# An encoder of two layers on one core: 128-row score products, the shared SBUF port in the second ordering, and the softmax's division on two heads' output

## The chip, the core and the metric

The kernel runs on one core of one Trainium2 chip. The core has five engines with queues of their own: TensorE (PE in the profile, with its weight loads shown apart as PEld), VectorE (DVE), ScalarE (ACT), GpSimd (POOL) and SyncE (SP), which here issues the transfers. The metric is device time in microseconds (us) from launch to end. Each engine takes its instructions strictly in the order in which they were issued to it; it waits for other engines by semaphores.

## The reference, cut to what matters

`x` is 256 tokens by 1024, float32. Each of two layers does this:

```python
h = rmsnorm(x, n1)
qa, ka, va, qb, kb, vb = split(h @ w_in)
# A: 8 query heads of 64 dims on 2 key/value heads, every token with every token
s = einsum('bqkgd,bskd->bkgqs', q, k) * scale
p = softmax(s); ya = einsum('bkgqs,bskd->bqkgd', p, v)
# B: 8 heads, three dilated windows, merged by their softmax denominators
y = concat(rmsnorm(ya, out_norm_a), rmsnorm(yb, out_norm_b))
x = x + y @ w_out
u = square(relu(rmsnorm(x, n2) @ w_mlp_in))
x = x + u @ w_mlp_out
```

A final rmsnorm ends the trunk. For B the kernel adds, to the scores, the logarithm of how many of the three windows a key is in; then one softmax does for all three.

## The kernel before, in words

**Products in split parts.** A float32 factor is held as two parts, `hi` (rounded to TensorE's fp32r) and `lo` (the rest). A product is three matmuls: hi·hi, hi·lo, lo·hi. Weights arrive by DMA in `wraw`, chunk by chunk into a ring of 4096 columns; `prep_piece` makes `whi` (a copy by ACT or DVE) and `wlo` (a subtraction by DVE, or by DVE or POOL for the chunks of the projections in `POOLK`, not for those of the MLP) in rings of 8192 columns, in pieces of mostly 640 or 384 columns. `block` is one such product of 128 weight columns with 256 tokens.

**Stages of a layer.** (1) q and k of A, outermost over the eight blocks of the model dimension. (2) V of all heads, with tokens on the partitions; between its products stand five `hooks` that finish q and k of A. (3) Attention of 16 heads, one `score(k)`, `turn(k-1)`, `pv(k-2)` at a time, with products between them that don't need it: `fill_pair` (q and k of a pair of B's heads) and `fill_wa` (A's part of the output projection). (4) B's part of the output projection (`fill_wb`, on banks 1, 5, 6 and 7), residual, second norm. (5) the MLP. In layer 1 the last product has its tokens on the partitions, and the final norm closes it.

**One head.** `QS[i]` holds a head's q with the hi part on 64 partitions and the lo part on the other 64. `k_split` writes a head's k: `ks[0]` has the hi part on both halves (two ACT copies), `ks[1]` has the lo part on one half alone (a DVE subtraction). `score` makes, for each half `th` of the queries, a matmul with 128 rows (q hi and q lo against k hi) and one with 64 rows (q hi against k lo). Then come the row maximum (DVE), the exponentials with their sums `ls` (ACT), `li` = 1/`ls` (DVE), and two instructions that scale the probabilities `p` by `li`, on POOL, DVE or ACT. `turn` transposes `p` on TensorE (four 128x128) and splits it into `h` (ACT) and `l` (DVE). `pv` multiplies by V; at the second head of a pair it adds the hi and lo rows into `y` (two DVE additions, after two ACT copies), sums its squares (POOL) and writes `yh` and `yl` for the output projection.

**What sets the order.** All engine calls go to a `Sequencer`, which records each instruction with its data dependences and an estimated duration (`cost`), and issues them at the end (`issue`) in the order of a list schedule. `order` runs twice. The first run chooses the engine where several can do a step; `PEN` holds penalties in ns by kind. The second run, with the engines fixed, gives the order of issue. `record` marks instructions that use the SBUF port shared by DVE and POOL: DVE's with two inputs in SBUF, DVE's SBUF-to-SBUF copies and scalings, and every POOL instruction that reads a tile. In the first run two such instructions may not overlap; for the second run `issue` empties this mark, so that they may. The order alone is changed by this: the semaphores come from the data. All engine instructions carry one source line (L368), so the profile's groups are told apart by the names of their tiles.

Of the kernel before, what the change touches and what calls it, by code (L numbers as in the profile page):

```python
# [19 lines left out]
NRAW = 4096     # columns of weights as they come  # L20
NHI = 8192      # and split
# [6 lines left out]
NIN0 = 3                              # pairs of ff blocks in the K-outer start of the MLP  # L28
LAG = 2
N_PAIR = 16  # L30
# what an engine's end counts more, in the choice among several, per kind of instruction
PEN = {"": {"POOL": -700}, "norm": {"POOL": -450, "ACT": 300}, "rot": {"POOL": -500}, "hi": {"DVE": 300}}


def plan():
    """The weights in chunks of some columns, in the order in which TensorE takes them."""
    out = []
    for l in range(L):
        out += [(("A", l, kb), 640) for kb in range(8)]
        out += [(("V", l, kb), 640) for kb in range(8)]  # L40
        out += [(("B", l, p, i), 1024) for p in range(4) for i in range(2)]
        out += [(("WA", l, i), 1024) for i in range(4)]
        out += [(("WB", l, p), 1024) for p in range(4)]
        out += [(("IK", l, kb), 256 * NIN0) for kb in range(8)]
# [63 lines left out]
def tables():  # L108
    """Constants that depend on shapes alone: rotary cosines and signed sines on
    [dim of two heads, token], the logarithms (times 8) of how many of the dilated  # L110
    patterns a key is in, the identity, and sums over a head or all."""
    f = np.float32
    tok = np.arange(S)
    d = np.arange(128) % 64
    fa = (f(10000.0) ** (-np.arange(16, dtype=f) / f(16))).astype(f)
    pos = np.where((d < 32)[:, None], (tok // 64)[None], (tok % 64)[None]).astype(f)
    ang = (pos * fa[d % 16][:, None]).astype(f).astype(np.float64)
    ca, sa = np.cos(ang), np.sin(ang) * np.where(d % 32 < 16, -1, 1)[:, None]
    fb = (f(500000.0) ** (-np.arange(8, dtype=f) / f(8))).astype(f)
# [16 lines left out]
class Sequencer:  # L136
    """Takes a kernel's instructions in program order, keeps what that order says
    of their data, and issues them in the order of a list schedule: each engine takes,
    of what is ready for it, what has the longest way to the end."""

    # from the end of one engine's instruction to the start of another's that waits for it
# [14 lines left out]
    def __getattr__(self, name):  # L156
        several = {"DP": ("DVE", "POOL"), "PDA": ("POOL", "DVE", "ACT"), "AD": ("ACT", "DVE")}
        if name not in ("PE", "ACT", "DVE", "POOL", "SP", *several):
            raise AttributeError(name)
        return _Recorder(self, several.get(name, (name,)))  # L160

    @staticmethod
    def form(e, method, args, kw):
        """An engine's instruction for what several engines can do."""
# [12 lines left out]
    def regions(ap, psum):  # L177
        """Where an access lies: partitions and spans of the free axis (a whole PSUM bank)."""
# [12 lines left out]
    def cost(e, method, outs, ins, kw):  # L191
# [6 lines left out]
        if e == "PE":  # L198
            f32 = ins[0].dtype == F32
            if kw.get("is_transpose") or method == "transpose":  # L200
                return 109
            return max(110, 1.7 * n) if f32 else max(109, 0.423 * n)
# [17 lines left out]
    def record(self, engines, method, args, kw):  # L220
# [28 lines left out]
        if engines == ("SP",):  # L249
            # the loads in program order  # L250
# [3 lines left out]
        # the SBUF port that DVE and Pool share  # L254
# [6 lines left out]
    def order(self):  # L261
# [31 lines left out]
        while done < n:  # L293
# [10 lines left out]
            if len(ops[i][0]) > 1:  # L304
                # the engine that ends it first
# [20 lines left out]
    def justify(self, start, end, succ):  # L326
        """Moves all instructions as late as they may be, then as early: gaps close."""
# [3 lines left out]
        for back in (True, False):  # L331
            busy = {e: [] for e in (*self.eng, "PORT")}     # spans, counted from this pass's beginning
# [28 lines left out]
    def issue(self):  # L361
        # once with the shared port, for the choice of engines, and once without
        self.order()
        self.ops = [([x for x in o[0] if x[0] == e], *o[1:5], {}, *o[6:]) for o, e in zip(self.ops, self.on)]
# [15 lines left out]
def trunk(ctx: ExitStack, tc: tile.TileContext, x, wts, prm, tab, fin, out):  # L380
    nc = tc.nc
    sq_ = Sequencer(nc)
    PE, ACT, DVE, POOL, SP, DP, PDA, AD = sq_.PE, sq_.ACT, sq_.DVE, sq_.POOL, sq_.SP, sq_.DP, sq_.PDA, sq_.AD
# [16 lines left out]
    # ---------------------------------------------------------------- tiles  # L400
# [21 lines left out]
    KA = [[T(f"ka{i}{s}", [128, S], F32R) for s in range(2)] for i in range(2)]  # L422
# [3 lines left out]
    tq = T("tq", [128, 2, S])             # gain-folded sines of q and k  # L426
    tb = T("tb", [128, 2, S])             # rs-folded tables of B
# [16 lines left out]
    # ------------------------------------------------------------- weights  # L444
# [6 lines left out]
    def places(total):  # L451
        """Each chunk's place in a circular buffer, and the last chunk that it overwrites."""
# [23 lines left out]
    def prep_piece():  # L476
        """Splits a piece of the next chunk, if its place is free."""
# [27 lines left out]
    def wgt(key, a, n, last=True):  # L505
        """(hi, lo) of n columns from a on in a chunk; with `last`, their last use."""
# [23 lines left out]
    def rowbc(c2, o):  # L530
        """o [128, 256] <- c2 [token, th] along the free axis on every partition."""
# [8 lines left out]
    def sums(l, ps):  # L540
        """From column sums of squares of x: mean square + eps, and its power -1/2."""
# [11 lines left out]
    # ---------------------------------------------------------------- start  # L553
    DVE.memset(ssx[:, 0:128], 0.0)
    # TensorE's clock rises while it waits for x
# [10 lines left out]
    DVE.memset(one, 1.0)  # L566
    x3 = x.rearrange("p (a b) -> p a b", a=KB)
# [46 lines left out]
    def norm_x(l):  # L614
        """norm's scale along the tokens, from the squares' sums."""
# [8 lines left out]
    # ---------------------------------------------------------------- layer  # L624
    for l in range(L):
        gA, gA2, gK, gK2 = P(l, 16), P(l, 17), P(l, 18), P(l, 19)
        # gain-folded tables
# [3 lines left out]
        # ---- q and k of A, K-outer behind the split of h  # L631
# [7 lines left out]
        # ---- V of all heads, tokens on the partitions, with the rest of A's q, k between  # L639
# [17 lines left out]
        def k_split(kh, kst_):  # L657
            """kst_[head][hi, lo]: each a head's 64 rows twice."""
# [15 lines left out]
        cq = cqt.rearrange("p (t h) -> p t h", t=2)   # scale of q's scores / 8  # L674
# [78 lines left out]
        # ---- attention of the 16 heads, with the products that don't need it between  # L753
# [31 lines left out]
        def heads(k):  # L785
            """stationary q, moving k (hi, lo) and the V pair of head k of 16."""
# [6 lines left out]
        def score(k):  # L793
            q, ks, _ = heads(k)
            a = slice(64 * (k % 2), 64 * (k % 2) + 64)
            b = v2(bank[k % 2])
            for th in range(2):
                mm(b[:, th], q[:, th * 128:(th + 1) * 128], ks[0], True, False)
                mm(b[:, th], q[a, th * 128:(th + 1) * 128], ks[1][a], False, True)
# [20 lines left out]
            for th in range(2):  # L820
                sq_.kind = "norm"
                PDA.scale(p[:, th], p[:, th], li[:, th:th + 1])
                sq_.kind = ""
# [16 lines left out]
        def pv(k):  # L840
# [10 lines left out]
            # rows of hi and lo parts together: a pair's y^T  # L851
# [7 lines left out]
            DVE.tensor_tensor(out=y[64:128], in0=bb[64:128, 1], in1=t_[64:128], op=ALU.add)  # L859
            ss = ssA if pr < 4 else ssB  # L860
# [68 lines left out]
        # ---- residual, norm2, MLP  # L929
# [37 lines left out]
        def mlp_out_t(ps_, banks=None):  # L967
            """W2 stationary: out^T."""
# [9 lines left out]
        # the last product's sums: half of the tokens, columns, bank  # L978
        outs = ((0, 0, 512, 1), (0, 512, 1024, 5), (1, 0, 512, 6), (1, 512, 768, 7), (1, 768, 1024, 4))

        def mlp_out_n(ps_, which=outs):
            """u^T stationary: out with tokens on the partitions."""
# [19 lines left out]
        def seed():  # L1002
            """The sums of the last product start from x, turned back."""
# [74 lines left out]
```

## Time and profile before

| | us |
|---|---|
| median of 3 runs | 632.05 |
| the three runs | 629.9, 632.05, 635.52 |
| span of the profiled execution (first to last instruction) | 630.3 |

For the profiled execution the span alone is given; it lies between the lowest of the runs and their median.

How to read the lines that follow: a group line gives engine, operation, output tile<-input tiles, shapes and xcount, then busy us and the mean ns of one, then the idle time of the engine before them and what ended it. A matmul's line gives `rows*columns` of the weights and then the moving shape. A line of the stretches view gives, for A:B in us, the length, the busy time of PE, PEld, DVE, ACT and POOL, each with its instruction count, then the granted TensorE clock as a share of full speed, the DMA engines' busy share and GB/s. A timeline line gives start, duration, engine, operation and tiles, and in brackets the engine's idle time before it with what ended that. Matmul durations overlap, since the engine is pipelined: the distance from start to start says what one costs.

### The profile page before, as it was taken

What the parts mean: (1) busy time and instruction counts of PE and PEld (TensorE: products, weight loads), DVE (VectorE), ACT (ScalarE), POOL (GpSimd) and SP (SyncE); (2) the same over time, 40 slices, a digit from 0 to 9 for tenths busy, and PEclk for the clock granted to TensorE, in tenths of its full rate; (3) what the DMA queues carried; (4) which work ended last, traced back from release to release, by engine and by line L of the source; (5) the groups of instructions that cost most, each with busy time, mean ns of one, the idle gap of its engine ahead of it and who ended that gap; (6) DMA issues with size and microseconds to landing.
All of it is one profiled execution on the core that took longest, in us unless ns stands there. A gap on an engine that the chain in (4) does not pass through costs nothing.

```text
span 630.3 us, 11899 instructions
## 1 busy us (share of the span) xinstructions
PE 611.6 (97%) x4500; PEld 576.6 (91%) x4500; DVE 483.9 (77%) x873; ACT 353.4 (56%) x723; POOL 181.9 (29%) x179
## 2 busy tenths in 40 slices
PE   8989999989999999999999999999999999999996
PEld 8988987989999999999999888898989999999995
DVE  6898899998986566666588879887988766667632
ACT  6567877865544444434464687786654444434412
POOL 1486885841000000000035766667300000000000
PEclk9979999999999999999999999999999999999999
DMA  7833111346674554645444301025568554544501
GB/s 262 275 150 134 68 68 34 130 139 201 251 251 167 203 186 151 222 177 178 141 151 134 135 35 68 34 74 173 158 242 297 204 205 156 221 180 149 186 1 67
DMA packets 29865, 98.58 MB, mean 156 GB/s; under 512 B 3440, under 2 KB 3952, under 8 KB 29808
## 3 DMA queue, kind: packets, MB, share of 16 engines
q1 hardware_dynamic: 29808, 97.82, 44.3%
q8 instruction: 35, 0.57, 0.3%
q14 instruction: 22, 0.18, 0.1%
HBM read 96.76 MB, written 1.05 MB: 155 GB/s over the span
## 4 chain that ended last, share of the span: by engine, by line
PE 65%; DVE 11%; issue 2%; ACT 1%; POOL 1%; POOLq 0%; ACTq 0%; DVEq 0%
PE bank L368 65%; DVE wlo L368 2%; DVE f L368 2%; DVE hl L368 2%; DVE qs L368 1%; DVE hst L368 1%; DVE xT L368 1%; DVE l L368 1%; DVE pr L368 1%; DVE kbt L368 0%; POOL sm L368 0%; ACT f L368 0%; ACT pr L368 0%; POOL f L368 0%; DVE yA__82 L368 0%
## 5 line engine op out<-in xcount | busy, mean ns | idle before, releaser
L368 ACT ACTIVATE whi<-wraw 128x640 fp32r<-128x640 f32 (+3 forms) x312 | 192.9, 643 | 171.3 <-PE bank L368 113.0
L368 DVE TENSOR_TENSOR wlo<-wraw,whi 128x640 fp32r<-128x640 f32 (+3 forms) x296 | 221.0, 777 | 64.7 <-ACT whi L368 63.5
L368 PE MATMUL bank<-hh,whi 128*128 128x256 f32 x784 | 222.4, 285 | 0.7 <-ACT whi L368 0.7
L368 PE MATMUL bank<-hl,whi 128*128 128x256 f32 x784 | 222.5, 285 | 0.6 <-DVE hl L368 0.5
L368 PE MATMUL bank<-hh,wlo 128*128 128x256 f32 x784 | 221.2, 285 | 0.1
L368 PEld LDWEIGHTS bank<-hh,whi 128*128 128x128 f32 x784 | 149.2, 191 | 2.4 <-ACT whi L368 1.2
L368 PEld LDWEIGHTS bank<-hl,whi 128*128 128x128 f32 x784 | 148.1, 189 | 1.4 <-DVE hl L368 1.2
L368 PEld LDWEIGHTS bank<-hh,wlo 128*128 128x128 f32 x784 | 147.3, 189 | 0.6 <-DVE wlo L368 0.3
L368 POOL TENSOR_TENSOR wlo<-wraw,whi 128x384 fp32r<-128x384 f32 (+1 forms) x49 | 66.8, 1375 | 161.1 <-DMA wraw<-in_w_dram 149.7
L368 PE MATMUL bank<-l,whi 128*128 128x256 f32 x256 | 72.4, 283 | 0.0
L368 PE MATMUL bank<-h,wlo 128*128 128x256 f32 x256 | 72.2, 282 | 0.0
L368 PE MATMUL bank<-h,whi 128*128 128x256 f32 x256 | 71.3, 280 | 0.0
L368 POOL TENSOR_TENSOR sm<-sm,mhalf 128x2 f32<-128x2 f32 (+2 forms) x12 | 11.8, 986 | 183.8 <-DVE sm L368 183.8
L368 PE MATMUL bank<-wlo,h 128*128 128x512 f32 (+1 forms) x160 | 56.1, 350 | 0.0
L368 PE MATMUL bank<-whi,l 128*128 128x512 f32 (+1 forms) x160 | 55.9, 349 | 0.0
L368 PE MATMUL bank<-whi,h 128*128 128x512 f32 (+1 forms) x160 | 55.8, 349 | 0.0
L368 PEld LDWEIGHTS bank<-h,whi 128*128 128x128 f32 x256 | 48.4, 190 | 0.0
L368 PEld LDWEIGHTS bank<-h,wlo 128*128 128x128 f32 x256 | 48.0, 188 | 0.0
L368 PEld LDWEIGHTS bank<-l,whi 128*128 128x128 f32 x256 | 47.9, 187 | 0.1
L368 POOL TENSOR_TENSOR ssx<-ssx,f 128x512 f32<-128x512 f32 (+1 forms) x22 | 27.6, 1253 | 48.7 <-ACT f L368 37.3
L368 ACT ACTIVATE h<-f 128x512 fp32r<-128x512 f32 x32 | 20.2, 631 | 28.1 <-DVE f L368 28.1
L368 DVE CAST whi<-wraw 128x640 fp32r<-128x640 f32 (+1 forms) x33 | 14.8, 452 | 26.9 <-PE bank L368 25.6
(113 smaller groups left out, 994.8 us busy)
## 6 DMA issues: line engine op xcount, KB each, us to landing
wraw<-in_w_dram SPq DMA_DIRECT2D x148, 512.0 KB, 3.7
wraw<-in_w_dram SPq DMA_DIRECT2D x31, 320.0 KB, 3.3
wraw<-in_w_dram SPq DMA_DIRECT2D x16, 384.0 KB, 3.3
tabt<-in_t_dram SPq DMA_DIRECT2D x1, 768.0 KB, 7.5
xT<-in_x_dram SPq DMA_DIRECT2D x1, 512.0 KB, 7.0
tabt<-in_f_dram SPq DMA_DIRECT2D x1, 512.0 KB, 7.0
out_dram<-f SPq DMA_DIRECT2D x1, 512.0 KB, 2.6
out_dram<-f SPq DMA_DIRECT2D x2, 256.0 KB, 2.2
```

The lines of the kernel that those rows point to most:

```text
L368: getattr(self.eng[e], method)(*args, **kw)
```

## The change

Four edits:

1. **Score products of 128 rows.** The half of `ks[1]` that held nothing is zeroed once, at the start, by four POOL memsets (for this the four `ka` tiles become one tile `KAt`), and the second score matmul runs over all 128 rows.
2. **The division.** The two scalings of `p` go. `li` is instead copied (DVE, SBUF to SBUF) for two heads into a 128x256 tile `cw`, 64 columns to each head; two TensorE transposes put it on the partitions of `y` in bank 7, and a DVE product scales `y`, before its squares are taken. The kind "norm" and its penalties go with it.
3. **The port kept in the order.** `issue` no longer empties the mark, so the second ordering too keeps DVE's and POOL's port instructions apart.
4. **A cost.** The estimated duration of an fp32r matmul of n columns goes from 0.423 n to 4 + 0.449 n ns (for 256 columns from 108 to 119).

```diff
+PEN = {"": {"POOL": -700}, "rot": {"POOL": -500}, "hi": {"DVE": 300}}
...
-            return max(110, 1.7 * n) if f32 else max(109, 0.423 * n)
+            return max(110, 1.7 * n) if f32 else max(109, 4 + 0.449 * n)
...
     def issue(self):
         self.order()
-        self.ops = [([x for x in o[0] if x[0] == e], *o[1:5], {}, *o[6:]) for o, e in zip(self.ops, self.on)]
+        self.ops = [([x for x in o[0] if x[0] == e], *o[1:]) for o, e in zip(self.ops, self.on)]
...
-    KA = [[T(f"ka{i}{s}", [128, S], F32R) for s in range(2)] for i in range(2)]
+    KAt = T("ka", [128, 2, 2, S], F32R)
+    KA = [[KAt[:, i, s] for s in range(2)] for i in range(2)]
...
+    for i in range(2):
+        b = slice(64 - 64 * i, 128 - 64 * i)
+        POOL.memset(KAt[b, i, 1].bitcast(F32), 0.0)
+        POOL.memset(KBt[b, :, i, 1].bitcast(F32), 0.0)
...
         def score(k):
             q, ks, _ = heads(k)
-            a = slice(64 * (k % 2), 64 * (k % 2) + 64)
             b = v2(bank[k % 2])
             for th in range(2):
-                mm(b[:, th], q[:, th * 128:(th + 1) * 128], ks[0], True, False)
-                mm(b[:, th], q[a, th * 128:(th + 1) * 128], ks[1][a], False, True)
+                for s in range(2):
+                    mm(b[:, th], q[:, th * 128:(th + 1) * 128], ks[s], s == 0, s == 1)
...
             DVE.reciprocal(li, ls)
-            for th in range(2):
-                sq_.kind = "norm"
-                PDA.scale(p[:, th], p[:, th], li[:, th:th + 1])
-                sq_.kind = ""
             PT[k] = p
...
             DVE.tensor_tensor(out=y[64:128], in0=bb[64:128, 1], in1=t_[64:128], op=ALU.add)
+            pd = bank[7][:, 0:256]
+            cw = f512()[:, :256]
+            DVE.tensor_copy(cw.rearrange("p (t h d) -> p t h d", t=2, h=2),
+                            hst[:, k - 1:k + 1, 3].rearrange("p h t -> p t h")[:, :, :, None]
+                            .to_broadcast([128, 2, 2, 64]))
+            for th in range(2):
+                PE.transpose(pd[:, th * 128:(th + 1) * 128], cw[:, th * 128:(th + 1) * 128], ident)
+            DVE.tensor_tensor(out=y, in0=y, in1=pd, op=ALU.mult)
             ss = ssA if pr < 4 else ssB
```

More of the change, by code (lines that the diff above doesn't have):

```diff
@@ L30 @@
 N_PAIR = 16
-PEN = {"": {"POOL": -700}, "norm": {"POOL": -450, "ACT": 300}, "rot": {"POOL": -500}, "hi": {"DVE": 300}}
+PEN = {"": {"POOL": -700}, "rot": {"POOL": -500}, "hi": {"DVE": 300}}
 def plan():
@@ L156, in __getattr__ @@
     def __getattr__(self, name):
-        several = {"DP": ("DVE", "POOL"), "PDA": ("POOL", "DVE", "ACT"), "AD": ("ACT", "DVE")}
+        several = {"DP": ("DVE", "POOL"), "AD": ("ACT", "DVE")}
         if name not in ("PE", "ACT", "DVE", "POOL", "SP", *several):
@@ L382, in trunk @@
     sq_ = Sequencer(nc)
-    PE, ACT, DVE, POOL, SP, DP, PDA, AD = sq_.PE, sq_.ACT, sq_.DVE, sq_.POOL, sq_.SP, sq_.DP, sq_.PDA, sq_.AD
+    PE, ACT, DVE, POOL, SP, DP, AD = sq_.PE, sq_.ACT, sq_.DVE, sq_.POOL, sq_.SP, sq_.DP, sq_.AD
     sb = ctx.enter_context(tc.tile_pool(name="sb", bufs=1))
```

## The prediction

> **What bounds the kernel now.** I read the page's engine totals, then stretches of the span, then the weight loads' start times, then the waits.
>
> ```profile
> span 630.3 us, 11899 instructions
> ...
> PE 611.6 (97%) x4500; PEld 576.6 (91%) x4500; DVE 483.9 (77%) x873; ACT 353.4 (56%) x723; POOL 181.9 (29%) x179
> ```
>
> TensorE is busy for 97%, but those are several stages:
>
> ```profile
> 0.00:10.00 10.00, 8.50 (x39) 8.21 (x40) 4.10 (x16) 5.95 (x11) 0.60 (x6) 1.00 0.71 214
> 36.60:44.00 7.40, 7.34 (x31) 7.33 (x32) 7.20 (x12) 5.95 (x13) 5.40 (x3) 0.54 0.22 74
> 46.20:121.70 75.50, 73.49 (x514) 64.33 (x513) 68.67 (x157) 61.56 (x161) 56.13 (x62) 1.00 0.22 76
> 350.70:425.90 75.20, 73.22 (x505) 63.78 (x504) 64.18 (x151) 59.43 (x158) 50.29 (x57) 1.00 0.21 74
> 146.90:340.70 193.80, 193.80 (x1608) 193.66 (x1608) 139.79 (x221) 88.83 (x149) 13.53 (x13) 1.00 0.55 192
> ```
>
> The last row, layer 0's MLP and the start of layer 1, has no gap in TensorE; the change has nothing there. The third and fourth rows are the two attentions. There PE is 97% busy, and DVE is next with 91% (68.67 of 75.50) and 85% (64.18 of 75.20). The second row, part of V's stage of layer 0, ran at 0.54 of the clock: 7.40 x 0.46 = 3.4 us lost.
>
> PE's busy time in attention is not all work:
>
> ```profile
> 351.94 1.12 PEld L368 LDWEIGHTS bank<-ka,qs 128*128 128x128 f32 x4
> 353.19 0.19 PEld L368 LDWEIGHTS bank<-hh,whi 128*128 128x128 f32 x1
> 353.30 0.19 PEld L368 LDWEIGHTS bank<-hl,whi 128*128 128x128 f32 x1
> 353.42 0.19 PEld L368 LDWEIGHTS bank<-hh,wlo 128*128 128x128 f32 x1
> ```
>
> ```profile
> L368 PE MATMUL bank<-ka,qs 64*128 64x256 f32 x32 | 12.2, 381 | 0.0
> L368 PE MATMUL bank<-kbt,qs 64*128 64x256 f32 x32 | 12.2, 381 | 0.0
> L368 PE MATMUL bank<-hh,whi 128*128 128x256 f32 x784 | 222.4, 285 | 0.7 <-ACT whi L368 0.7
> ```
>
> A head's four score products take 1.25 us from start to start (351.94 to 353.19); products of the same 256 columns with 128 rows follow each other in 0.12 us. Four of those would take 0.48, so 0.77 us of a head is lost, and the 64-row kind is the odd one (381 ns against 285): each way between 64 and 128 rows costs about 0.19 us.
>
> The other engines hold each other up:
>
> ```profile
> 102.83 1.56 POOL L368 TENSOR_TENSOR wlo<-wraw,whi 128x640 fp32r<-128x640 f32 x1
> 102.91 1.75 DVE L368 TENSOR_TENSOR qs<-f,qs 64x256 fp32r<-64x256 f32 x1
> ...
> 103.88 0.46 PEld L368 LDWEIGHTS bank<-idt,pr 128*128 128x128 f32 x4
> ...
> 104.31 0.19 PEld L368 LDWEIGHTS bank<-h,V 128*128 128x128 f32 x1
> ...
> 104.34 1.47 POOL L368 TENSOR_TENSOR xT<-f,xT 128x512 f32<-128x512 f32 x1
> ...
> 104.69 1.39 DVE L368 TENSOR_TENSOR kbt<-f,kbt 64x256 fp32r<-64x256 f32 x1
> ...
> 106.01 0.67 DVE L368 TENSOR_TENSOR l<-bank,h 128x512 fp32r<-128x512 f32 x1
> ...
> 106.74 0.39 PE L368 MATMUL bank<-l,V 128*128 128x256 f32 x1 [1.20 <-DVE l L368]
> ```
>
> Two small DVE subtractions end only after the POOL instruction beside them, the `l` that PE needs starts late, and PE stands idle for 1.20 us.
>
> **The change part by part.**
>
> *Score products of 128 rows.* 32 heads x 0.77 = 24.6 us less on TensorE, 12.3 in each attention. The lower bound is nothing (rival D). The four memsets (256 and 768 columns, twice) come at the start, where POOL is idle (0.60 us busy in the first 10, the first row above), and their tiles are needed no sooner than V's stage: nothing. If that cover were gone, 2048 columns at POOL's 543 ns for 256 (row below) would be 4.3 us.
>
> *The division.* Gone are 64 scalings:
>
> ```profile
> L368 POOL TENSOR_SCALAR pr<-pr,hst 128x256 f32<-128x256 f32 x42 | 22.5, 543 | 25.0 <-DVE hst L368 24.4 <-PE bank L368 0.6
> L368 ACT ACTIVATE pr<-pr,hst 128x256 f32<-128x256 f32 x54 | 26.5, 502 | 10.3 <-DVE hst L368 10.0
> L368 DVE COPY f<-sm 128x256 f32<-128x256 f32 x2 | 1.4, 689 | 0.5 <-POOL sm L368 0.5
> L368 DVE TENSOR_TENSOR f<-bank,f 128x256 f32<-128x256 f32 x2 | 0.8, 412 | 0.0
> L368 DVE TENSOR_SCALAR hst<-hst 128x2 f32<-128x2 f32 x16 | 7.3, 454 | 0.2
> L368 DVE RECIPROCAL hst<-hst 128x2 f32<-128x2 f32 x32 | 5.0, 158 | 1.9 <-ACT pr L368 1.6
> ```
>
> 42 were on POOL; of ACT's 54, 32 are B's exponentials and 22 scalings. None was on DVE. Added for each of 16 pairs: on PE two transposes, like the four that take 0.43 us from 103.88 to 104.31, so 0.108 each and 3.5 us in all; on DVE a product like `f<-bank,f` (0.41) and a copy like `f<-sm`, whose two cases are
>
> ```profile
> 29.46 1.08 DVE L368 COPY f<-sm 128x256 f32<-128x256 f32 x1
> ...
> 338.20 0.29 DVE L368 COPY f<-sm 128x256 f32<-128x256 f32 x1 [0.47 <-POOL sm L368]
> ```
>
> 0.29 alone, 1.08 while a POOL instruction ran. I take 0.5, nearer the free case, because POOL has less to do: 0.91 a pair, 7.3 us of DVE per attention (bounds 5.6 to 11.9). The page "SBUF — State Buffer" of the Trainium skill (section "SBUF: two separate sides") says that DVE and GpSimd share an exclusive lock, held for a whole instruction, and that an fp32 copy inside SBUF takes it too. The trace agrees in the 1.08 against 0.29; by this rule each of the 16 new copies can wait for a whole POOL instruction, which is rival C.
>
> The way of a head gets shorter by a scaling (0.54) between the exponentials and `turn`; that of a pair gets longer by the product (0.41). The copy waits only for `li`, known two heads earlier. What is behind the new transposes in PE's queue waits for the copy; I cost that at nothing, as the copy has that lead, and up to a copy's 1.08 where it hasn't.
>
> Bank 7: `fill_wb`'s six blocks there of the first three pairs, 6 x 3 x 0.12 = 2.1 us, now come after the last pair's division. I cost this at nothing, because PE already waits near there (1.60 below), which these can fill: bounds -1.6 to +2.1 a layer.
>
> ```profile
> 129.72 0.43 PE L368 MATMUL bank<-idt,sm 128*128 128x128 f32 x2 [1.60 <-POOL sm L368]
> ```
>
> *What DVE gets back.* POOL loses 12.7 and 9.8 us in the attentions, so it can take the weight pieces that DVE splits there:
>
> ```profile
> L368 DVE TENSOR_TENSOR wlo<-wraw,whi 128x640 fp32r<-128x640 f32 x5 | 5.6, 1122 | 0.0
> L368 POOL TENSOR_SCALAR pr<-pr,hst 128x256 f32<-128x256 f32 x23 | 12.7, 560 | 11.7 <-DVE hst L368 11.7
> ...
> L368 DVE TENSOR_TENSOR wlo<-wraw,whi 128x640 fp32r<-128x640 f32 x4 | 4.9, 1240 | 0.0
> L368 POOL TENSOR_SCALAR pr<-pr,hst 128x256 f32<-128x256 f32 x19 | 9.8, 522 | 13.4 <-DVE hst L368 12.8 <-PE bank L368 0.6
> ...
> L368 POOL TENSOR_TENSOR wlo<-wraw,whi 128x640 fp32r<-128x640 f32 x17 | 28.3, 1664 | 149.7 <-DMA wraw<-in_w_dram 149.7
> ```
>
> Five or four pieces at 1.66 are 8.3 or 6.7 us there, which fits; DVE is rid of 5.6 and 4.9 (bounds: nothing, and all).
>
> *The port in the order, and the new cost.* They add no instruction; they move them. How much DVE loses to POOL now shows in a 128x2 scaling that takes 454 ns where a reciprocal of 128x2 takes 158: 16 x 0.3 = 4.7 us; in `qs`, 16 at 688 ns, where the PSUM product of twice the partitions takes 412, 4.4 us; and `kbt`, 16 at 618, 3.3 us. That is 12.4 us, 6.2 per attention. Scalings are 12.7 of POOL's 56.13 us, 23%, and so 1.4 of the 6.2. Between 1.4 and 6.2 I take 2.5, near the lower end, as POOL fills up with the pieces again. An order can also be worse: below, -1 (one stall like the 1.20).
>
> ```profile
> L368 DVE TENSOR_TENSOR qs<-f,qs 64x256 fp32r<-64x256 f32 x16 | 11.0, 688 | 0.5
> L368 DVE TENSOR_TENSOR kbt<-f,kbt 64x256 fp32r<-64x256 f32 x16 | 9.9, 618 | 0.3
> ```
>
> V's stage of layer 0 has such a stall too; the half clock follows it:
>
> ```profile
> 34.26 0.30 PE L368 MATMUL bank<-whi,hl 128*128 128x320 f32 x1
> 36.66 1.64 PE L368 MATMUL bank<-idt,f 128*128 128x2 f32 x8 [2.10 <-DVE f L368]
> ```
>
> 2.1 + 3.4 = 5.5 us could go, with the right order; I take 2.0, a good third.
>
> **Sum.** DVE's load becomes 68.7 + 7.3 - 5.6 - 2.5 = 67.9 in layer 0 and 64.2 + 7.3 - 4.9 - 2.5 = 64.1 in layer 1. PE's becomes 73.5 - 12.3 + 1.7 = 62.9 and 62.6. So DVE is late next. At 95% of the stretch, between DVE's 91% now and the 97% of PE as the bound, the attentions take 71.5 and 67.5: 4.0 and 7.7 us less. With 2.0 for V's stage the span falls by 13.7, from 630.3 to 616.6. That execution lies 1.75 under the median of 632.05; on the median's footing, 618.
>
> **Rivals.**
>
> *A, TensorE's price comes out whole.* DVE stays below PE, as it would if most of the 6.2 went. For it: DVE is at 85% in layer 1. Against: its new 7.3. 632.05 - 24.6 + 3.5 - 5.5 = 605.5.
>
> *B, DVE eats it.* No piece moves and the port is no freer: loads of 76.0 and 71.5, at 97% 78.3 and 73.7: +2.8 and -1.5, so 633. For it: DVE's 91%. Against: POOL's 22.5 us that are freed.
>
> *C, slower: the copies are held up.* Each takes 1.08 behind POOL, and nothing is given back: +11.9 per attention, loads of 80.6 and 76.1, at 97% 83.1 and 78.4, so +7.6 and +3.2: 643. It decides from where an attention's net load on DVE exceeds 97% of its 75.5 or 75.2, that is 4.6 us more in layer 0. Against: POOL is at 74% now, and less then.
>
> *D, the rows aren't the cause.* The 128-row products keep their 0.31 us; only the 3.5 for the transposes is left: 635.5. Against: every other 128-row kind follows at 0.12. The page "TensorEngine Tiling (Array Packing)" of the Trainium skill (section "Theoretical Speedup") gives row tiling, for 64 rows or fewer, up to twice the speed, which speaks against the change: 64 products at half of 0.12, so 3.8 us that it would give up, and 639 by an estimate from it. The trace differs, with 0.31 for each step to or from 64 rows. The same page (section "Key Properties") has a drain at each change of mode, with which the trace agrees.
>
> **How the numbers follow.** The forecast gets 0.45, A 0.22, B 0.20, C 0.10, D 0.03. The forecast's own range is 610 to 627 (DVE's terms at their bounds). Measurement tells apart about 1%, 6.3 us: faster is below 625.7, which is A and nearly all of the forecast, 0.65; slower is above 638.4, C with a part of D and of B's upper end, 0.13; the rest, 0.22, is within. The range of 605 to 633 reaches from A to B and leaves out C and D.
>
> **What would show it.** Four score products in 0.5 us from start to start, and no 64-row group: the first step. DVE at over 93% of attention, PE below 90%: DVE as the next bound; PE at 97% again would be A. No `pr<-pr,hst` on POOL and more `wlo` there: the pieces moved. The new copies near 0.3 or near 1.1 us decide between the forecast and C. `hst` scalings near 158 ns: the port's share. The clock's row after 36 us: V's stage. I am wrong if attention takes over 75 us with the score products at 0.5.

## The result, and the profile after

| | us |
|---|---|
| before, median of 20 runs (lowest, highest) | 631.86 (629.37, 635.52) |
| after, median of 20 runs (lowest, highest) | 636.56 (634.76, 642.45) |
| ratio after/before, 95% interval | 1.008 (1.0057 to 1.0104) |
| predicted | 618 (605 to 633) |

The change made the kernel slower by 0.8%: 5 us, within the 1% that was counted as no change, and outside the predicted range. The first fence is from the page of the changed kernel, the second from its stretches view (A:B, length, then busy us and count of PE, PEld, DVE, ACT and POOL, then granted clock, DMA share, GB/s): the two attentions and the stretch between them.

```profile
span 635.3 us, 11950 instructions
...
PE 604.0 (95%) x4532; PEld 578.3 (91%) x4532; DVE 481.9 (76%) x902; ACT 346.3 (55%) x701; POOL 164.4 (26%) x144
```

```profile
41.00:115.40 74.40, 66.94 (x504) 61.67 (x503) 72.90 (x169) 59.65 (x154) 47.08 (x42) 0.98 0.24 78
355.30:433.10 77.80, 68.87 (x518) 64.38 (x517) 70.62 (x165) 58.01 (x150) 46.50 (x43) 0.96 0.26 86
115.40:355.30 239.90, 234.72 (x1895) 233.89 (x1894) 172.46 (x281) 113.69 (x197) 43.28 (x32) 0.98 0.53 175
```

The stretch between the attentions in the kernel before:

```profile
121.70:350.70 229.00, 226.86 (x1869) 226.10 (x1868) 173.48 (x274) 113.10 (x194) 34.00 (x26) 1.00 0.52 180
```

TensorE's busy time fell by 7.6 us and the span rose by 5.0. In attention PE is now at 90% and 89%, and DVE at 98% and 91%. Stage by stage, against the same stages of the kernel before (a stage of attention ends with its last product by V, so the last pair's division and PE's wait for it lie in the next stage):

| stage | before | after | difference | forecast |
|---|---|---|---|---|
| start to attention, layer 0 | 46.2 | 41.0 | -5.2 | -2.0 |
| attention, layer 0 | 75.5 | 74.4 | -1.1 | -4.0 |
| between the attentions | 229.0 | 239.9 | +10.9 | 0 |
| attention, layer 1 | 75.2 | 77.8 | +2.6 | -7.7 |
| the rest | 204.4 | 202.2 | -2.2 | 0 |

The first step did what it was to do. In the timeline of weight loads (start, duration), a head's four score products now take 0.48 us from start to start, 47.22 to 47.70:

```profile
47.22 0.54 PEld L368 LDWEIGHTS bank<-ka,qs 128*128 128x128 f32 x4
47.70 0.14 PEld L368 LDWEIGHTS bank<-idt,pr 128*128 128x128 f32 x1
```

The groups of the changed kernel (xcount, then busy us and mean ns) show what DVE got and what POOL took over:

```profile
L368 POOL TENSOR_TENSOR wlo<-wraw,whi 128x640 fp32r<-128x640 f32 x21 | 35.3, 1682 | 149.2 <-DMA wraw<-in_w_dram 146.5 <-PE bank L368 2.6
...
L368 DVE TENSOR_TENSOR qs<-f,qs 64x256 fp32r<-64x256 f32 x16 | 14.6, 914 | 0.4
...
L368 DVE TENSOR_TENSOR kbt<-f,kbt 64x256 fp32r<-64x256 f32 x16 | 10.2, 640 | 0.3
L368 DVE TENSOR_SCALAR hst<-hst 128x2 f32<-128x2 f32 x16 | 9.1, 572 | 0.1
...
L368 DVE COPY f<-hst 128x256 f32<-128x256 f32 x16 | 8.1, 507 | 0.0
...
L368 DVE TENSOR_TENSOR yt<-yt,bank 128x256 f32<-128x256 f32 x16 | 6.7, 418 | 0.6
```

POOL splits 21 of the 640-column pieces, where it split 17. The copy and the product cost what was forecast (0.5 and 0.41). But of the small instructions that lose to POOL several got longer, where they were to get shorter: `qs` from 688 to 914 ns, the 128x2 scaling of `hst` from 454 to 572. (Not all: `hl` went from 898 to 833.)

Another part of the loss is half clock. The end of layer 0's attention, first in the timeline (in brackets PE's idle time and what ended it), then in the stretches view with a stretch of layer 1:

```profile
116.02 3.19 POOL L368 TENSOR_TENSOR wlo<-wraw,whi 128x384 fp32r<-128x384 f32 x2
...
117.70 1.78 DVE L368 SCALAR_TENSOR_TENSOR hl<-yt,prmt,hh 128x256 fp32r<-128x256 f32 x1
...
120.29 0.96 DVE L368 TENSOR_TENSOR wlo<-wraw,whi 128x768 fp32r<-128x768 f32 x1
121.28 0.42 DVE L368 TENSOR_TENSOR yt<-yt,bank 128x256 f32<-128x256 f32 x1
121.75 0.39 PE L368 MATMUL bank<-hh,whi 128*128 128x256 f32 x1 [2.45 <-DVE yt L368]
```

```profile
122.30:129.10 6.80, 6.80 (x34) 6.80 (x33) 3.38 (x4) 0.98 (x2) 4.56 (x4) 0.50 0.00 2
159.80:163.20 3.40, 3.40 (x19) 3.40 (x18) 2.83 (x5) 1.61 (x3) 0.71 (x2) 0.51 0.00 0
409.00:415.80 6.80, 5.19 (x22) 4.79 (x23) 5.11 (x12) 3.73 (x13) 2.40 (x2) 0.50 0.00 0
```

`hl` (1.78 us) ends only after two POOL pieces of 1.6; a weight piece of DVE's own (0.96) follows before the product. So DVE's chain to the last division is late, and PE, which waits for bank 7, stands for 2.45 us. Then TensorE runs at half its clock for 6.80 us with no gap in its work: 3.4 us lost. In the third row PE is busy for 5.19 of the 6.80 us, so there 3.4 is the most that half clock can have cost. Over the whole span the cores view says the same:

```profile
core 0: 635.3 us, clock 0.983
```

635.3 x 0.017 is 10.8 us short of full clock, against 630.3 x 0.008 = 5.0 before. These 5.8 us more are as much as the whole rise of the span, though an upper bound, since PE also waits in such stretches. The other executions have the same: the clock's median is 0.983 in the 20 runs of the changed kernel and 0.993 in the 21 runs of the kernel before that were taken beside e13 (below). In the stretch between the attentions the 10.9 us are made up of about 26 more products of 0.12 (3.1), 3.1 more of idle PE (5.2 against 2.1), and half of 6.8 + 3.4 (5.1).

### The profile page after: what moved, and what is told of

The parts are those of the page before. It is cut to its first block, busy times and chain, and to the rows that moved or that the text cites. A ratio compares the mean times of both kernels' runs of the same rounds, so it can differ in the third digit from the quotient of the medians.

```text
span 635.3 us, 11950 instructions
## 1 busy us (share of the span) xinstructions
PE 604.0 (95%) x4532; PEld 578.3 (91%) x4532; DVE 481.9 (76%) x902; ACT 346.3 (55%) x701; POOL 164.4 (26%) x144
## 4 chain that ended last, share of the span: by engine, by line
PE 70%; DVE 16%; DMA 5%; ACT 5%; issue 2%; SPq 1%; POOL 0%; POOLq 0%; ACTq 0%; DVEq 0%
PE bank L368 70%; DMA wraw<-in_w_dram 4%; DVE hst L368 3%; DVE f L368 2%; DVE qs L368 2%; DVE yt L368 2%; DVE l L368 1%; ACT whi L368 1%; ACT pr L368 1%; DVE kbt L368 1%; DMA tabt<-in_t_dram 1%; DVE wlo L368 1%; SPq L368 1%; ACT f L368 1%; DVE pr L368 1%
## 5 line engine op out<-in xcount | busy, mean ns | idle before, releaser
L368 DVE TENSOR_TENSOR wlo<-wraw,whi 128x640 fp32r<-128x640 f32 (+3 forms) x292 | 205.6, 734 | 66.2 <-ACT whi L368 64.9
L368 PEld LDWEIGHTS bank<-hh,wlo 128*128 128x128 f32 x784 | 149.3, 191 | 0.2
L368 POOL TENSOR_TENSOR wlo<-wraw,whi 128x384 fp32r<-128x384 f32 (+1 forms) x53 | 70.3, 1345 | 153.7 <-DMA wraw<-in_w_dram 146.5
L368 PE MATMUL bank<-h,whi 128*128 128x256 f32 x256 | 71.5, 281 | 0.0
L368 POOL TENSOR_TENSOR ssx<-ssx,f 128x512 f32<-128x512 f32 (+1 forms) x22 | 31.0, 1410 | 60.7 <-ACT f L368 42.0
```

What stands on the lines that cost most here:

```text
L368: getattr(self.eng[e], method)(*args, **kw)
```

## The experiments

The edits are numbered as in the change: 1 rows, 2 division, 3 port in the order, 4 cost. Medians of 5 to 11 runs, each ratio against runs of the kernel before on the same chip (medians 632.2 to 633.2). The ratios stand as recorded; those of the medians are up to 0.4% away.

| run | what it is | us | ratio (95%) |
|---|---|---|---|
| e1_rows | 1 | 623.07 | 0.9827 (0.9778 to 0.9875) |
| e2_division | 2 | 643.13 | 1.0163 (1.0101 to 1.0225) |
| e3_port | 3 | 647.54 | 1.0199 (1.0140 to 1.0257) |
| e4_cost | 4 | 641.74 | 1.0126 (1.0073 to 1.0179) |
| e5_all_but_port | 1, 2, 4 | 639.81 | 1.0108 (1.0069 to 1.0147) |
| e6_all_but_division | 1, 3, 4 | 622.23 | 0.9834 (0.9791 to 0.9877) |
| e7_all_but_rows | 2, 3, 4 | 643.98 | 1.0173 (1.0127 to 1.0219) |
| e8_rows_division | 1, 2 | 640.59 | 1.0124 (1.0085 to 1.0162) |
| e12_rows_port | 1, 3 | 631.57 | 0.9988 (0.9955 to 1.0021) |
| e9_copy_on_act | after, copy on ACT | 629.37 | 0.9950 (0.9910 to 0.9989) |
| e10_no_division | after, no division at all | 630.37 | 0.9955 (0.9920 to 0.9990) |
| e11_last_pair_bank0 | after, last pair in bank 0 | 636.08 | 1.0086 (1.0053 to 1.0119) |
| e13_paced | after, POOL waits again | 626.71 | 0.9883 (0.9827 to 0.9940) |
| e14_no_division_paced | e10, POOL waits again | 619.38 | 0.9766 (0.9704 to 0.9827) |
| e18_pace_on_act | after, ACT has that instruction | 637.27 | 1.0082 (1.0048 to 1.0117) |
| e15_scalings_on_act | 1, 3, 4, scalings on ACT | 629.88 | 0.9920 (0.9882 to 0.9957) |
| e16_act_copy_bank0 | e9 and e11 | 629.31 | 0.9948 (0.9909 to 0.9986) |
| e17_paced_act_copy_bank0 | e9, e11 and e13 | 619.43 | 0.9794 (0.9752 to 0.9837) |

### Which edit costs

Each of the kernels e1 to e7 makes one edit, or leaves one out, with the hunks of the diff above; beside that only the tile `KAt` of the first edit stays in all of them.

Rows alone:

> The kernel before with the 128-row score products alone (the memsets with them). Both theories: the score products fall to about 0.5 us a head. Theory D (the division's DVE work is what ate the gain): nothing else is added to DVE, so much of the 24.6 us of TensorE comes out, 8 to 20 us faster (ratio 0.97 to 0.99). Theory O (the order with the port kept is what ate it): the same, 8 to 20 us faster. Rival N (attention was bound by DVE before as well, so that the steps between 64 and 128 rows were covered): less than 4 us.

```profile
43.50:117.10 73.60, 65.12 (x513) 61.41 (x512) 70.28 (x158) 60.96 (x161) 57.47 (x62) 1.00 0.25 85
346.50:416.00 69.50, 62.71 (x503) 60.06 (x502) 64.79 (x151) 58.66 (x158) 50.42 (x57) 1.00 0.24 78
```

623.07. In its stretches view (the two attentions) PE's busy time is 8.4 and 10.5 us less than before, where 12.3 was reckoned for each, and the stages are shorter by 1.9 and 5.7: DVE is then at 95% (70.28 of 73.60) and 93%. So a kernel whose PE has been relieved does come to DVE at about the 95% that the forecast took.

Division alone:

> The kernel before with the division moved alone: 64-row products and the second ordering without the port stay. Theory D: DVE gets 16 copies and 16 products, about 15 us by the durations in the changed kernel's profile, on engines that were at 91% and 85%: slower by 5 to 12 us. Theory O: within 4 us of before, since POOL's 22 us and a scaling on each head's way go.

643.13, +10.2 against 632.94, within the 5 to 12 of theory D.

The port alone, and the cost alone:

> The kernel before with the port kept in the second ordering, alone. Theory O: slower by 8 us or more, with small DVE instructions beside POOL's as long as before or longer, and PE waiting for DVE. Theory D: within 4 us of before.

> The kernel before with the new matmul cost alone (4 + 0.449 n). It moves three subtractions from POOL to DVE and two scalings from ACT to POOL, and else the order alone. Both theories: within 4 us of before, rather a little faster, because the estimate is nearer to the 0.12 us measured.

647.54 and 641.74, both slower, though neither adds an instruction. For the port this is theory O's time without its sign: the small DVE instructions got shorter (the table of sums further down). For the cost neither theory had it.

All but the port:

> The changed kernel with the second ordering free of the port again (edits 1, 2 and 4). The single edits gave -9.9, +10.2 and +8.8 us for these three. If they add up: +9, about 642 us. Theory O (the port in the order costs about 15 us wherever it stands): 622 us, as 637 less 15. Theory R (the ordering's estimates repair each other: with a longer matmul cost the list schedule runs other engines further ahead, so that single edits don't add up): within 5 us of the changed kernel's 637.

639.81, as theory R has it: the single edits don't add up. All but the division:

> The changed kernel with the probabilities scaled as before (edits 1, 3 and 4). Sum of the single edits: -9.9 + 14.6 + 8.8 = +13.5, about 646 us. Theory D (the division's DVE work is the cause): about 10 us under the changed kernel, 627. Theory R: between 627 and 640, the division's price being smaller where POOL and DVE are kept apart.

622.23, faster than any of the three had it. Its clock is as low as the changed kernel's (0.981 and 0.983, medians of the runs), so what the division costs against this kernel isn't half clock. All but the rows:

> The changed kernel with the 64-row product back (edits 2, 3 and 4). If TensorE were the bound in the changed kernel's attention, 24.6 us slower than it; if the rows bring there what they bring alone, 10 us slower, 647. If DVE bounds attention there and covers the steps, less than 5 us slower: 637 to 642.

643.98, 7.4 over the changed kernel, between the two answers that were named.

Rows with the division, and rows with the port:

> Before with 128 rows and the division moved (edits 1 and 2). Sum of the single edits: +0.3, so within 3 us of before. If the division makes DVE the bound, the rows are covered: 640 or more, near the division alone at 643.

> Before with the 128-row products and the port kept in the second ordering, old matmul cost (edits 1 and 3). Rows with port and cost gave 622, rows alone 623, port alone 648. If the port's price depends on the cost's estimate being right: 630 to 640. If the rows repair it: 620 to 625.

640.59, where rows covered by the division were to give 640 or more; and 631.57, where a port whose price depends on the matmul's estimate was to give 630 to 640.

What an edit is worth, as a difference of ratios in per cent (1% is 6.3 us):

| edit | alone | on other edits |
|---|---|---|
| rows | -1.7 | -0.4 on 2 (e8 - e2); -0.9 on 2, 3, 4 (after - e7); -2.1 on 3 (e12 - e3) |
| division | +1.6 | +3.0 on 1 (e8 - e1); +2.5 on 1, 3, 4 (after - e6) |
| port | +2.0 | +1.6 on 1 (e12 - e1); -0.3 on 1, 2, 4 (after - e5) |
| cost | +1.3 | -0.2 on 1, 2 (e5 - e8); -1.5 on 1, 3 (e6 - e12) |

The division costs wherever it is put in, and most where the rows have relieved PE. Without it (e6) the change makes the kernel 1.7% faster. The cost has no fixed sign, and the port goes from a loss of 2.0% to about nothing. The -0.2, -0.3 and -0.4 lie within the intervals of their two runs and can't be told from nothing.

### Which part of the division costs

The new copy goes from DVE to ACT:

```diff
-            DVE.tensor_copy(cw.rearrange("p (t h d) -> p t h d", t=2, h=2),
+            ACT.activation(cw.rearrange("p (t h d) -> p t h d", t=2, h=2),
                             hst[:, k - 1:k + 1, 3].rearrange("p h t -> p t h")[:, :, :, None]
-                            .to_broadcast([128, 2, 2, 64]))
+                            .to_broadcast([128, 2, 2, 64]), AF.Copy)
```

> The changed kernel with the copy of li into cw done by ACT and not by DVE. DVE loses 16 copies, 8.1 us by the changed kernel's profile; ACT (55% busy) gets them. Theory L (DVE's added load is the division's price): 5 to 8 us under the changed kernel, 629 to 632. Theory W (the price is the waits in order that the division puts into queues: PE's transposes behind the copy, bank 7 behind the product): less than 3 us under it, since the waits stay.

```profile
L368 ACT ACTIVATE f<-hst 128x256 f32<-128x256 f32 x16 | 6.6, 412 | 3.0 <-DVE hst L368 2.6 <-DVE qs L368 0.3
```

629.37: about 7 us come back, as theory L has it for 8.1 us of DVE. But the order is made anew here too, and other DVE instructions got shorter with it (`qs` 519 ns, 914 after), so the 7 us aren't the copy's own time alone.

The copy, the two transposes and the product are taken out and the scalings stay out, so `y` is that of undivided sums:

```diff
-            pd = bank[7][:, 0:256]
...
-            DVE.tensor_tensor(out=y, in0=y, in1=pd, op=ALU.mult)
```

> The changed kernel with the division left out altogether: no copy, no transposes, no product, and no scaling of the probabilities (the output is that of undivided softmax sums). Against the kernel with all edits but the division (622) it shows what the scalings of the probabilities cost, against the changed kernel (637) what the copy, transposes and product cost together. Theories L and W both: 12 to 20 us under the changed kernel, 617 to 625. If it stays above 630, neither: then it is the order that differs without the scalings.

630.37. This run decided against the first account, that the division costs by what it adds. With nothing added and the scalings gone the kernel is still 8 us above e6 (622.23), which does all the scalings. Something that the scalings did, or the order that is planned with them, is missed.

The last pair's product goes to bank 0, so that `fill_wb`'s blocks in bank 7 needn't wait for it:

```diff
-            pd = bank[7][:, 0:256]
+            pd = bank[7 if k < 15 else 0][:, 0:256]
```

> The changed kernel with the last pair's transposes put in bank 0 in place of bank 7, so that the last projection's products on bank 7 needn't wait for the last pair's product. Theory W: the 2.45 us wait of PE for yt at 121.75 goes, and the half clock after it (6.8 us, so 3.4 lost): 3 to 6 us under the changed kernel, 631 to 634. Theory L: less than 2 us, since DVE is as late as before.

```profile
121.83 0.35 PE L368 MATMUL bank<-idt,ssx 128*128 128x1 f32 x2 [2.74 <-DVE yt L368]
```

```profile
core 0: 632.7 us, clock 0.986
```

636.08 against 636.56: no difference. But the edit didn't remove the wait. In the timeline of this kernel PE still stands for `yt`, now 2.74 us and ahead of the squares' sums of the same pair, because DVE is as late as before, which is what theory L said. So the run shows that bank 7 alone isn't the cause of the wait; what the wait itself costs it can't show. The clock hardly gained (0.986, 0.983 after).

### What the scalings did

Theory Q: in POOL's in-order queue a scaling waited for DVE (24.4 of POOL's idle time in the row of `pr<-pr,hst` before), and the weight pieces behind it waited too. Without the scalings POOL runs through its pieces of 1.0 to 1.7 us as they arrive, and DVE, so the theory, meets them more often. To test it, POOL gets back an instruction that waits and does almost nothing, a multiplication of two columns of `p` by one:

```diff
             DVE.reciprocal(li, ls)
+            for th in range(2):
+                POOL.tensor_scalar(p[:, th, 0:2], p[:, th, 0:2], 1.0, 1.0, op0=ALU.mult, op1=ALU.mult)
```

> The changed kernel with a POOL instruction added for each half of a head, which multiplies two columns of the probabilities by 1 where the scalings stood: POOL's queue has to wait there for the exponentials again, at almost no work. Theory Q (the scalings, waiting in POOL's queue for DVE and ACT, kept POOL in step; without them it runs ahead with its weight pieces and holds DVE up): small DVE instructions beside POOL get shorter (hst scalings from 572 ns to under 400), PE's waits shrink, 4 to 10 us under the changed kernel's 637, so 627 to 633. Theory L (DVE's added load alone): 635 to 640.

```profile
L368 POOL TENSOR_SCALAR pr<-pr 128x2 f32<-128x2 f32 x64 | 16.8, 269 | 31.7 <-ACT pr L368 23.8 <-PE bank L368 7.8
...
L368 DVE TENSOR_TENSOR qs<-f,qs 64x256 fp32r<-64x256 f32 x16 | 10.1, 630 | 0.7 <-ACT qs L368 0.4
...
L368 DVE COPY f<-hst 128x256 f32<-128x256 f32 x16 | 6.0, 374 | 0.0
...
L368 DVE SCALAR_TENSOR_TENSOR hl<-yt,prmt,hh 128x256 fp32r<-128x256 f32 x8 | 4.4, 547 | 0.9 <-ACT hh L368 0.9
...
L368 DVE TENSOR_SCALAR hst<-hst 128x2 f32<-128x2 f32 x16 | 3.2, 202 | 0.1
```

626.71: 64 instructions more, and 10 us less. POOL's queue again waits 23.8 us for `pr`, and the DVE groups that met POOL are shorter: the copy 374 ns (507 after), `qs` 630 (914), `hl` 547 (833), `hst` 202 (572).

The same in the kernel without a division, whose output is again that of undivided sums:

> The kernel without any division (it gave 630) with the same two-column POOL instructions. Theory Q: near the 622 of the kernel with the scalings, 618 to 625. Theory L, which has nothing for the 8 us between the two: 628 to 633.

619.38, 11 us under e10.

The same instruction on ACT, so that POOL's queue gets nothing to wait for:

```diff
             DVE.reciprocal(li, ls)
+            for th in range(2):
+                ACT.activation(p[:, th, 0:2], p[:, th, 0:2], AF.Copy)
```

> The changed kernel with the two-column instructions on ACT in place of POOL: they lengthen a head's way in the list schedule as before, but POOL's queue has nothing to wait for. Theory Q (POOL's wait is what helps): 633 to 640, and DVE's hst scalings over 450 ns. Rival P (a longer way of a head makes the schedule start heads sooner, and this helps): 624 to 630.

```profile
L368 ACT ACTIVATE pr<-pr 128x2 f32<-128x2 f32 x64 | 11.6, 195 | 0.1
...
L368 DVE COPY f<-hst 128x256 f32<-128x256 f32 x16 | 8.3, 520 | 0.0
```

637.27, nothing comes back, and the copy is as long as ever. So it isn't the instruction as such, nor the delay that it puts on a head, that saves the 10 us: it has to stand in POOL's queue. The sign that was named failed, though: the scalings of `hst` took 399 ns here, not over 450, and `qs` 663; others were long in their place (the `yA__82` row of DVE 1135 ns, 713 after).

The other way round: the division left as it was (edits 1, 3 and 4), with all scalings on ACT, so that POOL loses its waits without a new instruction anywhere:

```diff
-                PDA.scale(p[:, th], p[:, th], li[:, th:th + 1])
+                ACT.scale(p[:, th], p[:, th], li[:, th:th + 1])
```

> Edits 1, 3 and 4 with the probabilities scaled on ACT alone, none on POOL (the kernel with 44 of them on POOL gave 622). ACT gets 44 more at 0.5 us, 22 us over two attentions in which it was busy for about 80%. Theory Q: without POOL's waits DVE is held up more (hst scalings over 450 ns), 628 to 636. If POOL's waits don't matter: 620 to 626.

629.88, 7.7 above e6. The time is as theory Q has it, but the sign that it named for `hst` failed: those scalings were short here, 190 ns. `qs` was long (799 ns, against 508 in e6). And ACT has more work here, so this run alone doesn't tell POOL's waits from ACT's load.

### The version that beats both

Without the waiting instruction, copy on ACT and bank 0; then with it:

> The changed kernel with both repairs: the copy on ACT (629 alone) and the last pair's transposes in bank 0 (636 alone). If they add up: 628 to 629. It can only beat 622 if the last pair's wait was hidden by DVE's lateness before: 620 or less.

> The changed kernel with the three repairs together: the two-column POOL instructions (627 alone), the copy on ACT (629 alone) and the last pair's transposes in bank 0 (636 alone, 629 with the copy). If they add up: 637 - 10 - 7 - 0 = 620, which would be near the kernel with edits 1, 3 and 4 (622). If the POOL wait already gave DVE the room that the copy would give: 625 to 628.

629.31 and 619.43: again 10 us between a POOL that waits and one that doesn't. The second is 2.1% faster than the kernel before and 17 us faster than the changed one: 7 from the copy and 10 from POOL's waits, about what the division had cost on the other edits (2.5%, 15.6 us). Its attentions in the stretches view, and then DVE's instructions on the tile `wlo` in each of them (min/median/max ns, first and last start):

```profile
44.80:115.30 70.50, 66.49 (x523) 62.73 (x523) 66.34 (x168) 62.63 (x164) 55.20 (x74) 1.00 0.29 95
347.00:416.40 69.40, 65.36 (x513) 61.45 (x513) 62.73 (x160) 59.12 (x157) 50.20 (x73) 1.00 0.28 93
```

```profile
L368 DVE TENSOR_TENSOR wlo<-wraw,whi x6: 817/1291/1715, 61.3 to 114.9; 128x640 fp32r<-128x640 f32 x4, 128x768 fp32r<-128x768 f32 x2
L368 DVE TENSOR_TENSOR wlo<-wraw,whi x6: 808/818/1617, 349.4 to 412.6; 128x640 fp32r<-128x640 f32 x6
```

The two attentions take 139.9 us together against 143.1 in e1, both at full clock, though DVE splits six weight pieces in each.

## Why the prediction was wrong

**Score products: right in mechanism, large in size.** Four can take 0.48 us. PE's busy time fell by 18.9 us in e1, where 24.6 was reckoned. The prediction took one head for all: 1.25 us before is among the dearest, 0.48 among the cheapest. The distances from each score product's start to the next product's, added over all 32 heads of the trace, are 37.9 us before and 18.5 in e1, so a head's price was 0.61 us and not 0.77. And e1 gained 9.9 us of the 18.9; DVE was at 95% and 93% there.

**DVE as the next bound: right, but for layer 1.** 95% and 93% in e1, 98% in layer 0 of the changed kernel. In its layer 1 DVE was at 91%, under the 93% that was named, and the stage took 77.8 us, over the 75 at which the prediction called itself wrong.

**The division's own price: right.** 8.1 + 6.7 = 14.8 us of DVE, 7.4 per attention against 7.3. The copies were not held up as rival C had it (mean 507 ns, not 1.08 us). That PE's queue would not wait for the copy held in the changed kernel (1.4 us of waits for it), but not where the division stands without the port: there PE waits, in the groups view of e8, for the copy and for the probabilities,

```profile
L368 PE MATMUL bank<-idt,f 128*128 128x128 f32 x36 | 7.9, 302 | 5.4 <-DVE f L368 5.4
L368 PE MATMUL bank<-idt,pr 128*128 128x128 f32 x128 | 24.7, 280 | 7.6 <-ACT pr L368 6.4 <-DVE l L368 1.1
```

and likewise in e2 and e5 (3.7 and 5.0 for the copy, 4.5 and 7.0 for the probabilities), where the kernel before and e1 have less than 1 us of either.

**What DVE gets back: this step failed.** It had two terms. The weight pieces on DVE, in each attention, before and after:

```profile
L368 DVE TENSOR_TENSOR wlo<-wraw,whi x6: 811/904/2176, 45.0 to 121.4; 128x640 fp32r<-128x640 f32 x5, 128x768 fp32r<-128x768 f32 x1
L368 DVE TENSOR_TENSOR wlo<-wraw,whi x4: 805/1248/1659, 350.1 to 370.8; 128x640 fp32r<-128x640 f32 x4
```

```profile
L368 DVE TENSOR_TENSOR wlo<-wraw,whi x1: 810/810/810, 63.1 to 63.1; 128x640 fp32r<-128x640 f32 x1
L368 DVE TENSOR_TENSOR wlo<-wraw,whi x3: 809/812/815, 359.5 to 428.1; 128x640 fp32r<-128x640 f32 x3
```

They did move: in layer 0 about as forecast, in layer 1 one of four (2.5 us of the 4.9). That is the smaller failure; e17 keeps six on DVE in each attention and is the fastest kernel that divides. What failed above all is the relief of 2.5 us per attention from POOL, with its reason that a POOL with less to do holds DVE up less. POOL did less, 47.08 us against 56.13 in layer 0, and held DVE up more. Six groups of small DVE instructions are the same 80 instructions in all kernels: `qs`, `kbt`, the two kinds on `hst`, `yA__82` and `hl`. Their rows in the groups view, added, went from 48.0 us before to 53.2 after, where relief of 5.0 was forecast. The prediction counted the scalings as work (23% of POOL's busy time) and their 24.4 us of waits as nothing; its own row showed the waits.

The same sum in all the kernels shows how far this goes:

| second ordering | POOL waits for the softmax | POOL doesn't |
|---|---|---|
| without the port | 48.0 before, 49.8 e1, 47.5 e4 | 45.7 e2, 47.8 e8, 45.6 e5 |
| with the port | 36.7 e3, 38.6 e12, 36.6 e6, 35.8 e13, 36.5 e14, 34.6 e17 | 53.2 after, 52.6 e7, 52.3 e11, 50.6 e18, 49.2 e10, 44.0 e15, 41.3 e16, 40.2 e9 |

With the port kept in the order every kernel whose POOL waits is under 39 us and every other is over 40. Without it there is no such step, though the division costs there too (e2, e8). So POOL's lost waits explain DVE's longer instructions only together with edit 3; without edit 3 the price shows in PE's waits above.

How it is held up can be seen in the durations of `hst`'s scalings in the tile view (min/median/max ns), before, after, and in e13:

```profile
L368 DVE TENSOR_SCALAR hst<-hst x16: 139/169/1422, 83.4 to 417.3; 128x2 f32<-128x2 f32 x16
```

```profile
L368 DVE TENSOR_SCALAR hst<-hst x16: 152/183/1524, 81.6 to 427.7; 128x2 f32<-128x2 f32 x16
```

```profile
L368 DVE TENSOR_SCALAR hst<-hst x16: 151/162/695, 78.5 to 414.7; 128x2 f32<-128x2 f32 x16
```

An instruction of two columns takes 0.15 us when it is free and up to 1.5 us, nearly a whole POOL piece, when it isn't. In the changed kernel each of the seven that took over 0.35 us ends 0.02 to 0.03 us after a POOL instruction. That is the exclusive lock of which the Trainium skill speaks ("SBUF — State Buffer", "SBUF: two separate sides"), and the trace agrees in this 1.5 beside the 1.6 of a piece. The longest in e13 is 0.7.

**The 95%, and bank 7 at nothing.** In layer 1 DVE's 70.62 us at 95% would be 74.3; the stage took 77.8. The half clock from 409.00 to 415.80 could be the other 3.5 (3.4 at most, as PE wasn't busy throughout); no run tells. The forecast had half clock only as something that could go, and it came back at other places. Nothing was forecast for the stretch between the attentions, where the largest miss of all stages lies, 10.9 us (layer 1's attention misses by 10.3). A wait near bank 7's bound came (2.45 us against 2.1), with 3.4 us of half clock behind it, which the bound left out. Behind it stands DVE's lateness and not bank 7 alone, as e11 shows.

**V's stage: right in sign, small.** 5.2 us went, nearly the 5.5 that could; 2.0 was taken.

**Of the rivals**, B was nearest ("DVE eats it"): its load of 76.0 and 71.5 against 72.90 and 70.62. What it lacked is that DVE could be held up more than before. In D, 0.31 us is what one of a head's four products took (1.25 / 4); the step between 64 and 128 rows is the 0.19 that the prediction has further up.

**What stays open.** Every edit also changes the whole order of issue, since the list schedule is made anew. Three pairs of kernels differ by POOL's waiting instruction alone (e13 and after, e14 and e10, e17 and e16) and all three by 10 or 11 us, while the control on ACT gives 0.7 the other way; but no run keeps the order and adds the wait alone, so the wait as such and the order that is planned around it were not told apart. Nor is the whole gain DVE's: in each pair the kernel that waits also has the higher clock (medians 0.988 against 0.983, 0.992 against 0.981, 0.997 against 0.989), so that up to 3 to 7 of the 10 or 11 us are half clock that it doesn't have. Why the port alone (+14.6 us) and the cost alone (+8.8) are slower was not settled: in e3 the six groups took 36.7 us, so there DVE was held up less. Up to 10 of its 14.6 us are half clock (0.976 against 0.992), but what brings that on is open.

## What to carry to other kernels

In a queue that is taken in order, a cheap instruction that waits is also a brake on what stands behind it: before it is removed from an engine that shares a resource, its waiting time counts, beside its busy time. Taking work from a side engine needn't be relief for the main one: here the main one was held up more, in an order that was planned to keep the two apart. And edits should be timed with and without each other: here the rows were worth 1.7% alone and less than 1% beside the division. Whether an edit has removed a wait is read from its trace and not from its time: in e11 the wait had only moved.

## What the runs showed of the hardware that was not expected

Half clock comes in stretches of 3.4 us or a multiple, after short waits of PE, and runs on through work without a gap. The three stretches shown above follow the 2.45 us at 121.75 and these rows of the timeline of the changed kernel:

```profile
159.38 0.43 PE L368 MATMUL bank<-idt,sm 128*128 128x128 f32 x2 [2.08 <-POOL sm L368]
...
404.26 0.38 PE L368 MATMUL bank<-yA__82,whi 128*128 128x256 f32 x1 [1.55 <-DVE yA__82 L368]
...
407.85 0.39 PE L368 MATMUL bank<-l,V 128*128 128x256 f32 x1 [1.17 <-DVE l L368]
```

The Trainium skill ("TensorE: Matmul & The Clock Gate", "HAM oscillation — how this bites in real kernels") gives as a rule that gaps over about 3.4 us are to be avoided. The half rate and the length of a stretch agree with that page; here gaps of 1.2 to 2.5 us were followed by half clock, though not every such gap was: in the kernel before, the 2.10 us ahead of 36.66 were, and the 1.60 us ahead of 129.72 were not.
